# Expert layer: two tiles routed before the first one-hots, dots of gathered rows spread over two tiles, four row buffers

## The chip, the cores and the metric

The kernel runs on 1 core of one Trainium2 chip. The metric is the device time in microseconds (us) of one launch. Engines are named as in the profile: PE is TensorE (PEld its weight loads), DVE is VectorE, ACT is ScalarE, POOL is GpSimd, SP issues transfers. All arithmetic is in float32; large products are split into a high and a low part (three matmuls in place of one).

## The reference, cut to what matters

The program runs two blocks of layers on 512 tokens of width 1024. The change lies in the last layer, a product-key expert layer (PEER) with 16,384 experts; each token takes 128 of them.

```python
def peer_ffn(h, wq, subkeys, u, v):
    q = (xt @ wq).reshape(T, PEER_HEADS, 2, PEER_HALF)
    s = jnp.einsum('thpc,hpnc->thpn', q, subkeys)
    s_top, i_top = lax.top_k(s, PEER_TOPK)
    cand = s_top[:, :, 0, :, None] + s_top[:, :, 1, None, :]
    cand_idx = i_top[:, :, 0, :, None] * PEER_N_KEYS + i_top[:, :, 1, None, :]
    best, pos = lax.top_k(cand.reshape(T, PEER_HEADS, -1), PEER_TOPK)
    experts = jnp.take_along_axis(cand_idx.reshape(T, PEER_HEADS, -1), pos, axis=-1)
    gates = jax.nn.softmax(best, axis=-1)
    ...
        ub = u[eb]
        vb = v[eb]
        act = jax.nn.gelu(jnp.einsum('cd,ced->ce', xb, ub)) * gb
        return jnp.einsum('ce,ced->cd', act, vb)
```

## The kernel before

The 512 tokens are four tiles of 128. Tile 0 and half of tile 1 (`HT = 64` tokens) are computed sparsely, from gathered rows of `u`; the other 320 tokens (`TU`) densely: products with all 16,384 rows of `u`, in 128 blocks of 128 experts, times a matrix G that holds the gates of the chosen experts and zeros elsewhere. Nothing of the dense products depends on the routing, so the first 66 blocks (`NA`) are computed during the routing and stored to memory (`up_store`, here "a fill": 24 matmuls at line 192, one GELU at line 1247, one store at line 1248; its weights come from SP, are split by ACT at line 115 and by POOL at line 118).

The part that the change touches is the last third of `peer`:

- `route(t, out)` (line 1257) finds for tile t the best 16 of each head's candidates and their expert numbers as two digits, nearly all of it on DVE; six operations of it (lines 1299, 1303, 1307, twice) are large, 128x2048 elements. Its PE part is none; one exponential runs on ACT.
- `transposed(res)` (line 1326) turns the two digits and the gates of a tile round: three PE transposes (line 1329) and a copy on ACT (line 1331) into `rt`.
- `onehots(t, rt, steps, pace, fills)` (line 1390) builds G for one tile in 32 groups of four tokens. A group needs two one-hot tiles, `oh1` (line 1405 on DVE, in one group of four line 1403 on POOL) and `oh2` (lines 1408 on DVE and 1410 on ACT, or 1413 and 1414 on DVE), four PE matmuls (line 1417) and a copy into `stage` on ACT (line 1419). After a group the function takes steps from the generator `steps` until they have used `pace` units per group, and it issues its share of `fills` fills. Tiles 2 and 3 are then written to memory (line 1433).
- `udots_begin`, `udots`, `udots_end` (lines 1350 to 1388) compute the sparse half of tile 1. `udots_begin` makes the row numbers `idx1` (line 1356, behind two small PE matmuls of line 1344) and the normalised tokens `xn1` (line 1367, behind the PE matmuls of line 1362 and a load of a gain row, line 1364). Then 64 gathers of 128 rows each (512 KB, `ugather`, line 1347, an indirect transfer issued by POOL) fetch rows of `u` into the row buffers `ub`, and 64 dots on DVE (line 1374) multiply them with `xn1` and sum. `xn1` and the three buffers lie in the dead activations `xT`, 4 KB per partition each.

The order of the work is the program's order: a Tile scheduler fills each engine's queue from it, each queue runs in order, and an operation waits for what it reads and for whoever still uses what it writes. The calls at the end of the section, in the order in which they stand (lines 1452 to 1460):

```python
        fill(FIRST)
        ...
        for _ in route(2, res):
            pass
        onehots(2, transposed(res), between2(), 3.1, 20)
        onehots(3, rts[0], between3(), 2.9, 20)
        onehots(1, rts[1], route(0, r0), 1.45, 12)
        fill(NA)
```

`between2` (line 1440) routes tile 1, starts the dots and routes tile 3 beside the one-hots of tile 2; `between3` (line 1448) computes the 64 dots beside those of tile 3; tile 0 is routed beside those of tile 1. After this the dense products run to the end of the launch.

Of the kernel before, what the change touches and what calls it, by code (L numbers as in the profile page):

```python
# [14 lines left out]
ALU = mybir.AluOpType  # L15
# [4 lines left out]
D = 1024  # L20
P = 128
# [6 lines left out]
FIRST = 14  # L28
# [15 lines left out]
def body(tc, A, out, upto=None, dbg=None):  # L44
    nc = tc.nc
# [1108 lines left out]
    def peer(norm):  # L1154
        H, L = norm.h, norm.l
        TD, TU, HT = 384, 320, 64
# [75 lines left out]
        def b_(name, shape, bufs=1, dt=F32):  # L1232
            return pgb.tile(list(shape), dt, name=name, tag=name, bufs=bufs)
# [18 lines left out]
        def fill(n):  # L1252
            for _ in range(n):
                if ahead:
                    up_store(ahead.popleft())
# [80 lines left out]
        xn1, ub = flat[:, 0:D], [flat[:, (n + 1) * D:(n + 2) * D] for n in range(3)]  # L1336
# [9 lines left out]
        def ugather(k):  # L1346
            G.indirect_dma_start(out=ub[k % 3], out_offset=None, in_=urows,  # L1347
                                 in_offset=bass.IndirectOffsetOnAxis(ap=idx1[:, k:k + 1], axis=0))

        def udots_begin(res):  # L1350
# [13 lines left out]
            nc.scalar.dma_start(ub[2], A["ffn_norm_row"].to_broadcast([P, D]))  # L1364
            for hf in range(2):
                o = slice(hf * 512, (hf + 1) * 512)
                V.tensor_tensor(xn1[:, o], pxs[hf], ub[2][:, o], ALU.mult)
            ugather(0)
            ugather(1)

        def udots():
            for k in range(HT):
                u = ub[k % 3]
                V.scalar_tensor_tensor(u, u, 1.0, xn1, op0=ALU.mult, op1=ALU.mult, accum_out=dval[:, k:k + 1])  # L1374
                if k + 2 < HT:
                    ugather(k + 2)
                yield 1.4
# [12 lines left out]
        def onehots(t, rt, steps, pace, fills):  # L1390
# [3 lines left out]
            for q4 in range(32):  # L1394
# [5 lines left out]
                oh1 = b_("oh1", (P, 4, P), bufs=3)  # L1400
# [5 lines left out]
                oh2 = b_("oh2", (P, 4, P), bufs=3)  # L1406
# [32 lines left out]

        def between2():  # L1440
            yield from route(1, r1)
            udots_begin(r1)
            yield 3.0
            res = []
            yield from route(3, res)
            rts.append(transposed(res))

        def between3():
            yield from udots()
            rts.append(udots_end(r1))  # L1450

        lsplit[:] = [G]
        fill(FIRST)
        res = []
        for _ in route(2, res):
            pass
        onehots(2, transposed(res), between2(), 3.1, 20)
        onehots(3, rts[0], between3(), 2.9, 20)
        onehots(1, rts[1], route(0, r0), 1.45, 12)
# [336 lines left out]
```

## Time and profile before

| | |
|---|---|
| median of 3 runs | 2993.33 us (2985.81 to 2994.05) |
| the profiled execution | 2987.53 us, its span 2985.8 us |
| PE busy | 2857.4 us, 96% of the span |
| DVE, ACT, POOL busy | 2006.1, 1430.8, 1244.9 us |
| granted clock of PE, mean | 0.984 |
| transfers | 516.84 MB, 173 GB/s |

The rows used below come from the page of the profiled execution and from queries of its trace. A row of a stretch (a window of the span) gives each engine's busy time (PE, PEld, DVE, ACT, POOL) and, in brackets, its instructions, then the granted clock as a share of the full 2.4 GHz, the busy share of the DMA engines and GB/s. A row of waits gives who waited, for whom, the total, how often and the longest. A row of a timeline gives start, duration, engine, line and operation, and in square brackets the idle time of the engine ahead of it with its releaser. Matmuls are pipelined, so the duration of one is longer than the distance to the next.

### The profile page before, as it was taken

To read this page: it belongs to the slowest core of one execution; us is meant where nothing else is said; L and a number is where in the kernel's file an instruction comes from. 1 tells how busy PE (TensorE), PEld (TensorE's weight loads), DVE (VectorE), ACT (ScalarE), POOL (GpSimd) and SP (SyncE) were. 2 spreads that over 40 slices of the span, in tenths; PEclk is the share of its full clock that TensorE was granted. 3 is DMA by queue.
4 is the path that set the end of the run, shared out by engine and by line. 5 is a ranking of instruction groups with operands and counts; after the bars stand their busy time and mean duration, and the time that the engine had idled before them with its cause. 6 is when DMAs were issued, how large, how long until landed. Compare 5 with 4: busy or idle time off the path is not lost.

```text
span 2985.8 us, 47379 instructions
## 1 busy us (share of the span) xinstructions
PE 2857.4 (96%) x18255; PEld 2561.3 (86%) x18255; DVE 2006.1 (67%) x3484; ACT 1430.8 (48%) x2464; POOL 1244.9 (42%) x800
## 2 busy tenths in 40 slices
PE   8999999999999999999999998866799999999998
PEld 8999999988899998875788898866788888888887
DVE  4656645567664647447655778677867888887887
ACT  4454433366542435425444346634575545555555
POOL 4124323342232324105312355577655555555553
PEclk9999999999999999999999999987999999999999
DMA  4213322331132233221242344789758999999996
GB/s 134 66 51 100 100 97 95 100 99 43 64 100 93 99 100 108 85 71 41 71 130 88 107 137 142 201 277 290 214 223 328 353 364 348 356 358 351 349 352 238
DMA packets 216002, 516.84 MB, mean 173 GB/s; under 512 B 83032, under 2 KB 120280, under 8 KB 198880
## 3 DMA queue, kind: packets, MB, share of 16 engines
q1 hardware_dynamic: 172320, 325.29, 33.1%
q0 software_dynamic: 27648, 167.78, 14.9%
q10 hardware_dynamic: 15808, 20.74, 2.0%
q8 instruction: 143, 2.34, 0.3%
q14 instruction: 83, 0.68, 0.1%
HBM read 481.96 MB, written 31.78 MB: 172 GB/s over the span
## 4 chain that ended last, share of the span: by engine, by line
PE 77%; DVE 6%; issue 5%; POOL 5%; ACT 3%; DMA 3%; SPq 0%; ACTq 0%; DVEq 0%; POOLq 0%
PE mm L192 60%; PE ax L192 11%; POOL wl L118 2%; POOL xT L1347 2%; PE ax L1417 1%; DMA xT<-in_uv_dram,idx 1%; DVE scr L1530 1%; ACT wh L115 1%; POOL oh L1403 1%; DVE xt L1539 1%; PE mm L1027 1%; PE ax L1211 1%; DMA w<-in_pv_dram 1%; DVE xT L1374 0%; PE ax L997 0%
## 5 line engine op out<-in xcount | busy, mean ns | idle before, releaser
L118 POOL TENSOR_TENSOR wl<-w,wh 128x1024 fp32r<-128x1024 f32 x265 | 665.0, 2511 | 956.3 <-ACT wh L115 769.7
L115 ACT ACTIVATE wh<-w 128x1024 fp32r<-128x1024 f32 (+1 forms) x530 | 559.1, 1057 | 717.6 <-PE mm L192 443.2
L192 PE MATMUL mm<-sh,wh 128*128 128x256 f32 (+2 forms) x3144 | 746.9, 303 | 7.1 <-ACT sh L225 6.4
L192 PE MATMUL mm<-sl,wh 128*128 128x256 f32 (+2 forms) x3144 | 743.5, 302 | 1.9 <-POOL sl L205 1.7
L192 PE MATMUL mm<-sh,wl 128*128 128x256 f32 (+2 forms) x3144 | 742.1, 301 | 1.1 <-DVE wl L118 1.1
L192 PEld LDWEIGHTS mm<-sh,wh 128*128 128x128 f32 (+1 forms) x3144 | 498.1, 188 | 40.4 <-ACT sh L225 6.4
L192 PEld LDWEIGHTS mm<-sl,wh 128*128 128x128 f32 (+1 forms) x3144 | 497.0, 188 | 32.3 <-POOL sl L205 2.0
L192 PEld LDWEIGHTS mm<-sh,wl 128*128 128x128 f32 (+1 forms) x3144 | 497.5, 188 | 30.4 <-DVE wl L118 1.4
L118 DVE TENSOR_TENSOR wl<-w,wh 128x1024 fp32r<-128x1024 f32 (+1 forms) x265 | 339.4, 1281 | 234.0 <-ACT wh L115 228.5
L192 PE MATMUL mm<-xnh,wh 128*128 128x320 f32 x784 | 256.3, 327 | 2.0 <-ACT wh L115 2.0
L192 PE MATMUL mm<-xnh,wl 128*128 128x320 f32 x784 | 252.0, 321 | 3.0 <-POOL wl L118 3.0
L192 PE MATMUL mm<-xnl,wh 128*128 128x320 f32 x784 | 252.9, 323 | 0.0
L1417 PE MATMUL ax<-oh,oh 128*128 128x128 f32 x768 | 130.9, 308 | 80.9 <-ACT oh L1410 42.8
L1417 PEld LDWEIGHTS ax<-oh,oh 128*128 128x128 f32 x768 | 112.3, 208 | 98.0 <-ACT oh L1410 52.0
L285 DVE TENSOR_TENSOR xT<-xT,mm 128x512 f32<-128x512 f32 x80 | 54.7, 686 | 163.3 <-PE mm L192 163.3
L192 PE MATMUL mm<-wh,ah 128*128 128x512 f32 x384 | 152.4, 397 | 9.5 <-ACT ah L1572 9.4
L192 PEld LDWEIGHTS mm<-xnh,wh 128*128 128x128 f32 x784 | 155.7, 199 | 3.7 <-ACT wh L115 2.2
L192 PEld LDWEIGHTS mm<-xnh,wl 128*128 128x128 f32 x784 | 155.1, 198 | 3.6 <-POOL wl L118 3.5
L192 PEld LDWEIGHTS mm<-xnl,wh 128*128 128x128 f32 x784 | 155.4, 198 | 1.3
L1419 ACT ACTIVATE stage<-ax 128x512 f32<-128x512 f32 x96 | 103.5, 1094 | 108.8 <-PE ax L1417 108.3
L192 PE MATMUL mm<-wh,al 128*128 128x512 f32 x384 | 151.9, 396 | 0.0
L192 PE MATMUL ax<-wh,ah 128*128 128x512 f32 x384 | 150.1, 391 | 0.0
(501 smaller groups left out, 5516.4 us busy)
## 6 DMA issues: line engine op xcount, KB each, us to landing
w<-in_pu_dram SPq DMA_DIRECT2D x128, 512.0 KB, 4.3
w<-in_pv_dram SPq DMA_DIRECT2D x128, 512.0 KB, 7.1
w<-in_up_dram SPq DMA_DIRECT2D x88, 512.0 KB, 3.5
w<-in_down_dram SPq DMA_DIRECT2D x48, 512.0 KB, 3.5
Gd<-stage SPq DMA_DIRECT2D x32, 512.0 KB, 8.1
gm<-Gd SPq DMA_DIRECT2D x128, 128.0 KB, 7.3
Hd<-gel ACTq DMA_DIRECT2D x66, 160.0 KB, 3.5
gst<-Hd SPq DMA_DIRECT2D x66, 160.0 KB, 7.2
```

The costliest lines, as they stand in the source:

```text
L115: SC.activation(h[:, :n], w[:, :n], AF.Copy)
L118: ins = eng.tensor_tensor(l[:, :n], w[:, :n], h[:, :n].bitcast(F32), ALU.subtract)
L192: PE.matmul(ps[:, c:c + w], lhsT=a, rhs=b[:, c:c + w], start=start and c == 0 and a is lh and b is rh, stop=stop and c + w == n and a is ll)
L285: V.tensor_tensor(xT[:, c], xT[:, c], ps, ALU.add)
L1027: PE.matmul(po[e * 64:e * 64 + 64, c * P:], lhsT=vs[:, c, hd * 64:hd * 64 + 64], rhs=at[:, c * P:], start=c == 0, stop=c == 3)
L1211: PE.matmul(pss[:, t * P:(t + 1) * P], lhsT=q[:, t * P:(t + 1) * P], rhs=sk, start=True, stop=True)
L1347: G.indirect_dma_start(out=ub[k % 3], out_offset=None, in_=urows, in_offset=bass.IndirectOffsetOnAxis(ap=idx1[:, k:k + 1], axis=0))
L1403: G.tensor_scalar(oh1[:, k], iot, rt[:, 0, 4 * q4 + k:4 * q4 + k + 1], None, op0=ALU.is_equal)
L1417: PE.matmul(pg[:, k * P:(k + 1) * P], lhsT=oh1[:, k], rhs=oh2[:, k], start=True, stop=True)
L1419: SC.activation(st[:, :, o:o + 4].rearrange("p j t -> p t j"), pg.rearrange("p (t j) -> p t j", t=4), AF.Copy)
L1530: V.scalar_tensor_tensor(scr, uv[:, :D], 1.0, xn, op0=ALU.mult, op1=ALU.mult, accum_out=d)
L1539: V.scalar_tensor_tensor(xt0, uv[:, D:], d, xt0, op0=ALU.mult, op1=ALU.add)
```

## The change

Tile 1 is routed first, then `udots_begin` is called and tile 2 is routed, all before the first one-hots; 21 fills (`FIRST`) stand ahead of this in place of 14, and 16 and 17 fills beside tiles 2 and 3 in place of 20 and 20. The dots are one generator that is drawn on beside tile 2's one-hots (with the routing of tile 3, 1.3 units of dots for one of routing) and beside tile 3's (with the routing of tile 0, 1.6 to one, and then the rest). Nothing is left to do beside tile 1's. `xn1` gets a tile of its own, so that `xT` holds four row buffers, and a gather is issued three dots ahead of its use in place of two. `oh1` and `oh2` have four buffers each in place of three.

```diff
-FIRST = 14
+FIRST = 21
...
-        xn1, ub = flat[:, 0:D], [flat[:, (n + 1) * D:(n + 2) * D] for n in range(3)]
+        xn1, ub = b_("xn1", (P, D)), [flat[:, n * D:(n + 1) * D] for n in range(4)]
...
         def ugather(k):
-            G.indirect_dma_start(out=ub[k % 3], out_offset=None, in_=urows,
+            G.indirect_dma_start(out=ub[k % 4], out_offset=None, in_=urows,
...
-            nc.scalar.dma_start(ub[2], A["ffn_norm_row"].to_broadcast([P, D]))
+            nc.scalar.dma_start(ub[3], A["ffn_norm_row"].to_broadcast([P, D]))
             for hf in range(2):
                 o = slice(hf * 512, (hf + 1) * 512)
-                V.tensor_tensor(xn1[:, o], pxs[hf], ub[2][:, o], ALU.mult)
-            ugather(0)
-            ugather(1)
+                V.tensor_tensor(xn1[:, o], pxs[hf], ub[3][:, o], ALU.mult)
+            for k in range(3):
+                ugather(k)
 
         def udots():
             for k in range(HT):
-                u = ub[k % 3]
+                u = ub[k % 4]
                 V.scalar_tensor_tensor(u, u, 1.0, xn1, op0=ALU.mult, op1=ALU.mult, accum_out=dval[:, k:k + 1])
-                if k + 2 < HT:
-                    ugather(k + 2)
+                if k + 3 < HT:
+                    ugather(k + 3)
                 yield 1.4
...
-                oh1 = b_("oh1", (P, 4, P), bufs=3)
+                oh1 = b_("oh1", (P, 4, P), bufs=4)
...
-                oh2 = b_("oh2", (P, 4, P), bufs=3)
+                oh2 = b_("oh2", (P, 4, P), bufs=4)
...
+        dots = udots()
+
+        def with_dots(steps, share):
+
+            owed = 0.0
+            for c in steps:
+                yield c
+                owed += share * c
+                while owed >= 1.4:
+                    owed -= 1.4
+                    d = next(dots, None)
+                    if d is not None:
+                        yield d
+
         def between2():
-            yield from route(1, r1)
-            udots_begin(r1)
-            yield 3.0
             res = []
-            yield from route(3, res)
+            yield from with_dots(route(3, res), 1.3)
             rts.append(transposed(res))
 
         def between3():
-            yield from udots()
+            yield from with_dots(route(0, r0), 1.6)
+            yield from dots
             rts.append(udots_end(r1))
 
         lsplit[:] = [G]
         fill(FIRST)
+        for _ in route(1, r1):
+            pass
+        udots_begin(r1)
         res = []
         for _ in route(2, res):
             pass
-        onehots(2, transposed(res), between2(), 3.1, 20)
-        onehots(3, rts[0], between3(), 2.9, 20)
-        onehots(1, rts[1], route(0, r0), 1.45, 12)
+        onehots(2, transposed(res), between2(), 2.35, 16)
+        onehots(3, rts[0], between3(), 2.6, 17)
+        onehots(1, rts[1], iter(()), 0.0, 12)
```

How the instructions now stand, at three places. A row gives the line of the kernel, the operation, what it writes from what it reads, and its size; x3 at a row's end is three in a row; a number behind a name tells tiles of one name apart.

On PE, at the end of the fills that stand ahead of the first one-hots; before, only the transposes of tile 2 (line 1329) stood between the last fill's matmul and the first one-hot product:

```order
L192 MATMUL mm<-xnh,wl 128x320
L1329 MATMUL ax<-ident,e_18383 128x128
L1329 MATMUL ax<-ident,e_18388 128x128
L1329 MATMUL ax<-ident,gt 128x128
L1417 MATMUL ax<-oh_18405,oh_18403 128x128 x2
```

and now the matmuls of `udots_begin` stand there too, behind 21 fills; the first of them (line 1344) makes the row numbers from the digits of tile 1, the last of them (line 1329) need the routing of tile 2:

```order
L192 MATMUL mm<-xnh,wl 128x320
L1344 MATMUL ax<-pf,ident 64x64 x2
L1344 MATMUL ax<-prcol,ident 64x2 x2
L1362 MATMUL ax<-ident,xT 64x128 x8
L1362 MATMUL mm<-ident,xT 64x128 x8
L1329 MATMUL ax<-ident,e_18741 128x128
L1329 MATMUL ax<-ident,e_18746 128x128
L1329 MATMUL ax<-ident,gt 128x128
L1417 MATMUL ax<-oh_18763,oh_18761 128x128 x4
```

The matmuls of lines 1344 and 1362 have moved from the middle of tile 2's one-hots to a place ahead of them.

On DVE, in the routing of tile 2, now: the row numbers (line 1356, `idx`, which reads what PE's line 1344 wrote) stand behind the small operations of this routing and ahead of its six large ones:

```order
L1317 TENSOR_TENSOR gt<-gt,sm 128x128
L1278 CAST pf<-bi 128x128
L1356 TENSOR_SCALAR idx_17833<-ax 128x64
L1357 COPY rdup<-ax 128x2
L1289 SCALAR_TENSOR_TENSOR fi<-pf,fi 128x128
L1290 SCALAR_TENSOR_TENSOR fj<-fi,pf 128x128
L1292 SCALAR_TENSOR_TENSOR fw<-fi,pf 128x128
L1299 TENSOR_TENSOR oh<-fi,ax 128x2048
L1293 SCALAR_TENSOR_TENSOR fj<-fw,fj 128x128
L1303 TENSOR_TENSOR oh<-oh,ax 128x2048
L1367 TENSOR_TENSOR xn_17832<-ax,xT 128x512
L1367 TENSOR_TENSOR xn_17832<-mm,xT 128x512
```

Behind these rows come four more large operations, four small ones and then the first one-hot. Before, nothing in the routing of tile 2 read anything of PE.

On DVE, in the middle of the dots, before (line 1374 is a dot; the one-hots are tile 3's):

```order
L1374 SCALAR_TENSOR_TENSOR xT,dval<-xT 128x1024 x2
L1414 TENSOR_TENSOR oh_20259<-mm,rt 128x512
L1374 SCALAR_TENSOR_TENSOR xT,dval<-xT 128x1024 x2
L1405 TENSOR_TENSOR oh_20275<-rt,ax 128x512
L1374 SCALAR_TENSOR_TENSOR xT,dval<-xT 128x1024
L1408 TENSOR_TENSOR oh_20277<-rt,ax 128x512
```

and now, where the one-hots are tile 2's and the other rows belong to the routing of tile 3:

```order
L1374 SCALAR_TENSOR_TENSOR xT,dval<-xT,xn_17832 128x1024 x2
L1408 TENSOR_TENSOR oh_19431<-rt,ax 128x512
L1303 TENSOR_TENSOR oh<-oh,ax 128x2048
L1405 TENSOR_TENSOR oh_19444<-rt,ax 128x512
L1413 TENSOR_TENSOR mm<-rt,ax 128x512
L1405 TENSOR_TENSOR oh_19494<-rt,ax 128x512
L1414 TENSOR_TENSOR oh_19446<-mm,rt 128x512
L1374 SCALAR_TENSOR_TENSOR xT,dval<-xT,xn_17832 128x1024 x2
L1408 TENSOR_TENSOR oh_19496<-rt,ax 128x512
L1307 TENSOR_REDUCE e_19508<-oh 128x128
```

The dots stand further apart: 29 of the 64 now lie ahead of the last one-hots of tile 2, the other 35 ahead of the last of tile 3.

## Rows read from the trace of the kernel before

**Rows 1.** The page: busy time of PE over the span.
```profile
PE 2857.4 (96%) x18255; PEld 2561.3 (86%) x18255; DVE 2006.1 (67%) x3484; ACT 1430.8 (48%) x2464; POOL 1244.9 (42%) x800
```

**Rows 2.** Stretches: first fills, then the one-hots of tiles 2, 3 and 1.
```profile
1757.00:1802.00 45.00, 43.87 (x300) 43.62 (x299) 29.35 (x101) 21.50 (x32) 30.56 (x14) 1.00 0.64 198
1802.00:1925.00 123.00, 108.58 (x752) 104.63 (x753) 106.64 (x272) 83.09 (x143) 68.27 (x57) 0.94 0.54 158
1925.00:2130.00 205.00, 140.76 (x766) 129.46 (x765) 146.87 (x198) 80.90 (x137) 152.13 (x116) 0.83 0.85 271
2130.00:2214.00 84.00, 76.51 (x556) 73.19 (x555) 68.01 (x166) 69.17 (x125) 44.88 (x40) 1.00 0.56 157
```

**Rows 3.** Waits of DVE in tile 3's stretch, 1925 to 2130.
```profile
DVE xT L1374 <- DMA xT<-in_uv_dram,idx: 57.6, 33, 7.9
```

**Rows 4.** Waits of DVE in tile 2's stretch, 1802 to 1925.
```profile
DVE oh L1405 <- ACT rt L1331: 15.6, 1, 15.6
DVE oh L1405 <- PE ax L1417: 13.5, 5, 5.8
```

**Rows 5.** The chain that ended last, from the first fills (start us, us, what).
```profile
1752.73 47.77 PE mm L192 x326
...
1801.86 0.39 ACT rt L1331
```

**Rows 6.** DVE's timeline: first and last operation of tile 2's routing, first one-hot.
```profile
1758.09 0.41 DVE L1259 CAST ax<-ti 128x256 f32<-128x256 uint32 x1
...
1782.05 2.29 DVE L1303 TENSOR_TENSOR oh<-oh,ax 128x2048 f32<-128x2048 f32 x1
1784.37 2.29 DVE L1307 TENSOR_REDUCE e<-oh 128x128 f32<-128x2048 f32 x1
1802.27 0.69 DVE L1405 TENSOR_TENSOR oh<-rt,ax 128x512 f32<-128x512 f32 x1 [15.61 <-ACT rt L1331]
```

**Rows 7.** Row buffers (tile xT), 1925 to 2130: waits (us, times); gathers' landing.
```profile
  issue: 6.7, 27
...
  POOL xT L1347: 41.8, 30
...
DMA to landing us min/median/max: 4.2/6.0/8.4
```

**Rows 8.** DVE's groups in tile 3's stretch: the dots (busy us, mean ns).
```profile
L1374 DVE SCALAR_TENSOR_TENSOR xT<-xT 128x1024 f32<-128x1024 f32 x62 | 104.7, 1695 | 57.8 <-DMA xT<-in_uv_dram,idx 57.6
```

**Rows 9.** Timeline about 1956: a dot beside a POOL split, undisturbed ones, one-hots.
```profile
1955.35 2.36 POOL L118 TENSOR_TENSOR wl<-w,wh 128x1024 fp32r<-128x1024 f32 x1
...
1956.42 2.38 DVE L1374 SCALAR_TENSOR_TENSOR xT<-xT 128x1024 f32<-128x1024 f32 x1 [0.90 <-DMA xT<-in_uv_dram,idx]
...
1962.57 0.68 DVE L1405 TENSOR_TENSOR oh<-rt,ax 128x512 f32<-128x512 f32 x1
1963.17 0.69 DVE L1413 TENSOR_TENSOR mm<-rt,ax 128x512 f32<-128x512 f32 x1
...
1970.81 1.22 DVE L1374 SCALAR_TENSOR_TENSOR xT<-xT 128x1024 f32<-128x1024 f32 x1
...
1971.95 1.22 DVE L1374 SCALAR_TENSOR_TENSOR xT<-xT 128x1024 f32<-128x1024 f32 x1
```

**Rows 10.** POOL's groups in tile 3's stretch, 1925 to 2130.
```profile
L1347 POOL DMA_INDIRECT xT<-in_uv_dram,idx x61 | 68.8, 1127 | 50.3 <-DVE xT L1374 41.8 <-issue 6.7 <-PE mm L192 0.8
L118 POOL TENSOR_TENSOR wl<-w,wh 128x1024 fp32r<-128x1024 f32 x22 | 53.0, 2410 | 0.5
L1403 POOL TENSOR_SCALAR oh<-iot,rt 128x128 f32<-128x128 f32 x33 | 30.8, 943 | 0.5 <-ACT rt L1331 0.3
```

**Rows 11.** POOL's groups in tile 2's stretch, 1802 to 1925.
```profile
L118 POOL TENSOR_TENSOR wl<-w,wh 128x1024 fp32r<-128x1024 f32 x19 | 45.8, 2420 | 36.0 <-ACT wh L115 35.9
```

**Rows 12.** The chain: one group's PE products at full clock.
```profile
2146.90 0.89 PE ax L1417 x8
```

**Rows 13.** Timeline: the end of the last fill's matmuls.
```profile
2213.50 0.31 PE L192 MATMUL mm<-xnh,wl 128*128 128x320 f32 x1
```

## The prediction

> **What bounds the kernel now.** I read the page first. PE is busy 96% of the span [rows 1], so the kernel can only gain where PE waits or runs at a lower clock. Of the page's slices it is those of the expert layer's one-hots that drop. I cut that stage into stretches [rows 2]: in the first fills PE is busy 43.87 of 45 us at full clock; beside tile 2's one-hots 108.58 of 123; beside tile 3's only 140.76 of 205, at a granted clock of 0.83; beside tile 1's 76.51 of 84. The reader should see that 205 us of tile 3 hold as many one-hots as the 123 us of tile 2, and much the same number of fills.
>
> The waits tell why. In tile 3's stretch DVE stands 57.6 us for gathered rows [rows 3], and POOL in turn stands 41.8 us for dots that have not yet given a row buffer back [rows 7]. It is one ring: a gather takes 6.0 us to land (median, 4.2 to 8.4 [rows 7]), its dot about 1.2 [rows 9], and with three buffers a gather may start only when the dot three places earlier is done. Since all one-hots stand in DVE's queue among the dots, they wait too, and PE behind them. In tile 2's stretch DVE loses 15.6 us at the start, because the transposes of tile 2 stand on PE behind the fills, and 13.5 us for one-hot buffers that PE has not yet read [rows 4].
>
> Everything after the stage is the same in both kernels; I take it to move as a block. So the sum is: when does the first one-hot of tile 2 start (before: 1802.3 [rows 6]), how long do tiles 2 and 3 take (before: to 2130, 327.7 us), how long does tile 1 take (before: 2130 to the last fill's end at 2213.8 [rows 13], 83.8 us).
>
> **The start.** 326 matmuls of the first fills take 47.77 us [rows 5], 0.1465 us each, 3.52 us for a fill of 24. By the order, 20.58 fills now stand in that place: 72.4 us from 1752.7, to 1825.1. DVE needs 28.6 us for one routing (1758.1 to the end of the last large operation, 1786.7 [rows 6]). Two would be done at 1815 and be hidden. But in DVE's queue the row numbers stand in the middle of tile 2's routing, and they read PE's line 1344, which stands behind all 21 fills. So DVE arrives there at about 1797 and stands until 1825.7. Behind it are six large operations at 2.3 us start to start [rows 6], 13.5 us, two `xn1` halves at 0.6 and eight small operations at some 0.25: 17 us, to about 1843. PE has nothing to do from 1826.5 on but the transposes that wait for this. Transposes and copy cost 1.8 us (before: 1800.5 to 1802.3 [rows 5, 6]), and I allow 1 us for small operations that POOL holds up: first one-hot at **1846**, 43.7 us later than before. The gain row lands well before `xn1` needs it; if it did not, 2 to 4 us more. Bounds: 1844 to 1850. Of this, 24.6 us are fills that only moved; the other 19 are PE standing still, and they have to be earned back.
>
> **Tiles 2 and 3.** The same work as before lies in this stretch: 64 groups of one-hots, 64 dots, two routings (3 and 0 in place of 1 and 3). From 327.7 us go:
> - 2 us for `idx1` and `xn1`, now ahead of it.
> - The wait for gathers, 57.6 us [rows 3]. With four buffers a gather waits for the dot four places earlier, and the dots are thinned out. Adding DVE's own starts along the new order (a dot 1.15, a one-hot operation 0.60 [rows 9], a large one 2.3 [rows 6]), four dots in a row span 9.8 us at the least and 12.8 in the median. A gather needs 1.2 for that dot and 6.0 to land, 7.2 us. That leaves 2.6 to 5.6 us for POOL to come round to it; a split of weights on POOL holds it for 2.41 [rows 10]. Most gathers land in time; I leave 5 us, bounds 0 and 25.
> - The wait for one-hot buffers, 13.5 us [rows 4]. Four buffers and a slower pace of one-hots: 5 left, bounds 0 and 13.5.
> - The stretching of dots. 62 dots took 104.7 us [rows 8]; at 1.22 undisturbed they would take 75.6, so 29 us are lost. The timeline shows to what: the dot at 1956.42 takes 2.38 us beside a POOL split that ends at 1957.71, while undisturbed ones start 1.14 apart [rows 9]. In tile 3's stretch POOL's tensor work was 53.0 + 30.8 us of 205 [rows 10], about 73 without its own stretching (33 one-hots at 0.6), 36%. Now the dots meet 33 splits and 64 POOL one-hots, 79 + 38 = 117 us of about 270, 43%: 29 becomes 36, **7 us more**. Bounds: 14 less (dots that no longer start on a buffer's return meet POOL at other moments) to 14 more.
>
> The Trainium skill says that a VectorE instruction with two SBUF inputs and a GpSimd instruction that reads SBUF exclude each other for a whole instruction, the first one wins (SBUF — State Buffer, Who interferes with whom). By that rule the dots, which read two such tiles, are the wrong work to lay beside more POOL work: it speaks against this change, and the 7 us stand. Without it the 29 us would stay and the gain be 7 larger. The 2.38 us row agrees with the rule.
>
> A second rule bears on the gathers: the Trainium skill has a POOL transfer cost about 2.0 us plus its bytes at 436 GB/s (DMA: Bandwidth & Descriptors, Anatomy of one DMA). By that estimate 512 KB land in 3.2 us; then no gather would be late in the new order and the 5 us left above be 0. The trace has 6.0 us, and I stay with it.
>
> Together: 327.7 − 2 − 57.6 + 5 − 13.5 + 5 + 7 = **271.6 us**, to 2117.6. A check from below: 64 groups of 2.25 DVE operations at 0.60 are 86 us, 64 dots at 1.15 are 74, two routings 57: 217 us with nothing in the way, plus 36 of stretching and some 16 of waits. PE's own work there, 33 fills at 3.52 and 64 groups at 0.89 [rows 12], is 173 us at full clock, 208 at tile 3's 0.83 [rows 2]: it stays covered by DVE, and so costs nothing as long as DVE takes longer.
>
> **Tile 1.** By the order 12.4 fills and 32 groups remain on PE: 43.6 + 28.5 = 72 us. DVE no longer has a routing there (28.6 of its 68.01 us [rows 2]), so PE sets the pace; ACT, busy 69.17 us before with the exponential of a routing, is just below it. I take **76 us**, bounds 72 and 84, to 2193.6.
>
> **Sum.** The stage ends at 2193.6 in place of 2213.8: 20.2 us earlier. The profiled execution took 2987.53 us for a span of 2985.8, so it would give 2967.3; the median of the runs is 5.8 us above that execution, and 2993.3 − 20.2 = **2973 us** is what I predict for the median.
>
> **The rivals.**
> - *POOL becomes the bound (slower).* In the new stretch POOL has 64 gathers at 1.13, 33 splits at 2.41 and 64 one-hots at up to 0.94 [rows 10], 72 + 80 + 60, and about 0.25 us of issue per gather (6.7 over 27 [rows 7]), 16: 228 us. If its splits also wait for ACT as they did in tile 2's stretch, 35.9 us in 123 [rows 11], that is 79 us in 271, and gathers queue behind those waits: 307 us. The stage would end at 1846 + 307 + 76 = 2229, 15 us later than before, **3008 us**. It decides from 292 us on (2213.8 − 76 − 1846). Against it: such a wait is mostly POOL being ahead with its splits, and a gather that stands behind one has 2.6 to 5.6 us to spare. For it: POOL's queue is in order, and 33 splits now lie among 64 gathers. Chance 0.12.
> - *The waits shrink but stay (no change).* Gathers are late by 15 to 25 us and the one-hot wait stays at 10 to 13.5: in place of 5 and 5 that is 15 to 28.5 us more in the stretch, so 5 us faster to 8 us slower, **2988 to 3002 us**. This is where the late start is just earned back. For it: the landing time reaches 8.4 us [rows 7], and the shortest four dots leave no room for that and a split. Chance 0.13.
> - *The new order does better (larger gain).* No late gathers, no one-hot waits, the stretching 15 us less than now, tile 1 at 72: 20 + 5 + 5 + 14 + 4 = 48 us, **2945 us**. For it: the dots come no longer right behind a gather's landing. Against it: all of this at once was seen nowhere in the trace. Chance 0.17 for over 33 us.
> - *The change does not do what it says.* Half of this is in the forecast: two tiles are routed ahead of the one-hots, but the second half of the second stands behind the fills.
>
> **How the numbers follow.** The forecast, a gain of 9 to 33 us, has 0.58. About 0.3%, 9 us, is what a measurement of this kernel can tell from no change. Faster by more than that: 0.58 + 0.17 = 0.75. Within it: 0.13. Slower: 0.12, the POOL case. The range goes from the larger gain's end, 2945, to 3000, near the upper end of no change; the slower case lies outside it.
>
> **What would show it.** In the new profile the first one-hot of tile 2 should start near 1846, with DVE standing some 28 us before `idx1` (waiting for line 1344) and PE some 18 us before line 1329. DVE's wait for gathers should fall below 10 us; the mean of a dot should stay at 1.7 to 1.8 us; tiles 2 and 3 should take 262 to 282 us and tile 1 72 to 80. I am wrong if the wait for gathers stays above 25 us, if POOL is full through the stretch, or if PE's clock falls so far there (below 173 / 292 = 0.59) that PE sets the pace.

## The result and the profile after

The changed kernel takes 2964.89 us (median of 5 runs, 2963.02 to 2987.88); on the same chip the kernel before takes 2994.05 us (median of 5, 2985.81 to 3005.99). The ratio is 0.992, with a 95% interval of 0.9895 to 0.9945: faster by about 24 us by the ratio and 29.2 us by the medians, where 20.2 us and a median of 2973 us were forecast.

The profiled execution of the changed kernel took 2987.88 us, 23 us above its median, with a span of 2986.1 us: it came to the first fills 12.4 us later than that of before, in code that both kernels share. So I compare stages here, cut at the same four points in every trace:

- the start: from the start of the last matmul of line 1211 (the product that the routing reads) to the start of the first one-hot of tile 2;
- tiles 2 and 3: from there to the multiplication on DVE that ends `udots_end`;
- tile 1: from there to the first transpose of the next stage on PE (line 1507 of the kernel before, 1522 of the changed one), which is 7 to 10 us beyond the end of the last fill, where the prediction ended it.

| kernel | start | tiles 2 and 3 | tile 1 | sum | median us | ratio, 95% interval |
|---|---|---|---|---|---|---|
| before | 49.8 | 326.8 | 94.8 | 471.4 | 2994.05 | |
| changed | 96.3 | 276.0 | 85.0 | 457.3 | 2964.89 | 0.992 [0.9895, 0.9945] |
| e1 the same, other chip | 96.0 | 266.9 | 84.9 | 447.8 | 2973.77 | 0.9924 [0.99, 0.9948] |
| e2 eight fills later | 78.1 | 267.4 | 84.9 | 430.4 | 2952.55 | 0.9874 [0.9851, 0.9897] |
| e3 three row buffers | 95.4 | 268.6 | 87.6 | 451.6 | 2970.08 | 0.9916 [0.99, 0.9933] |
| e4 dots from PSUM | 95.5 | 266.1 | 86.2 | 447.8 | 2962.26 | 0.9904 [0.9878, 0.9929] |
| e5 dots not spread | 95.8 | 288.1 | 83.4 | 467.3 | 2988.3 | 0.9985 [0.9976, 0.9994] |
| e6 before, four row buffers | 49.8 | 328.0 | 97.3 | 475.1 | 2984.66 | 0.9976 [0.9967, 0.9985] |
| e7 stores spread | 96.1 | 260.7 | 84.9 | 441.7 | 2958.25 | 0.9887 [0.9872, 0.9902] |
| e8 = e4 + e7 | 95.1 | 237.8 | 83.6 | 416.5 | 2936.89 | 0.9824 [0.981, 0.9837] |
| e9 = e8 + e2 | 78.2 | 242.9 | 83.6 | 404.7 | 2919.05 | 0.9759 [0.9746, 0.9773] |
| e10 three one-hot buffers | 95.6 | 267.7 | 85.0 | 448.3 | 2964.2 | 0.9906 [0.9892, 0.9921] |
| e11 = e9, dots not spread | 78.1 | 259.4 | 84.2 | 421.7 | 2943.92 | 0.9834 [0.9807, 0.9861] |

Stages come from the profiled execution of each kernel, medians from all its runs. The ratio is against the kernel before on the same chip.

The stretches of the changed kernel, with the columns of [rows 2]: up to the first one-hot of tile 2, tiles 2 and 3, tile 1 to the end of the last fill.

```profile
1750.00:1861.00 111.00, 91.04 (x616) 86.88 (x614) 71.60 (x294) 42.77 (x61) 61.29 (x28) 0.93 0.53 173
1861.00:2137.00 276.00, 210.57 (x1298) 197.09 (x1299) 251.17 (x462) 154.47 (x264) 203.45 (x156) 0.89 0.78 239
2137.00:2216.00 79.00, 78.03 (x585) 76.67 (x585) 45.05 (x74) 68.95 (x128) 47.34 (x44) 1.00 0.68 190
```

In tiles 2 and 3 DVE is now busy 251.17 of 276 us (91%); before it was 253.5 of 328 (106.64 + 146.87, 77% [rows 2]): the same work with fewer holes. In the last row PE is full, 78.03 of 79 us, where it had 76.51 of 84.

The start, by the waits of DVE from 1757 to 1861, and of PE in the same window:

```profile
DVE pf L1278 <- PE ax L1344: 28.4, 1, 28.4
...
DVE xn L1367 <- DMA xT<-in_ffn_norm_row_dram: 3.6, 1, 3.6
```

```profile
PE ax L1329 <- DVE e L1307: 18.7, 2, 11.4
```

DVE's timeline shows the end of this chain, from the release by line 1344 to the first one-hot:

```profile
1839.01 0.23 DVE L1278 CAST pf<-bi 128x128 f32<-128x128 uint32 x1 [28.35 <-PE ax L1344]
1839.15 0.21 DVE L1356 TENSOR_SCALAR idx<-ax 128x64 int32<-128x64 f32 x1
...
1848.39 0.69 DVE L1367 TENSOR_TENSOR xn<-ax,xT 128x512 f32<-128x512 f32 x1 [3.64 <-DMA xT<-in_ffn_norm_row_dram]
...
1861.19 0.69 DVE L1405 TENSOR_TENSOR oh<-rt,ax 128x512 f32<-128x512 f32 x1 [1.31 <-ACT rt L1331]
```

DVE stands one operation ahead of the row numbers: line 1278 writes `pf`, a tile with one buffer into which line 1353 has put tile 1's expert numbers, and line 1344 has yet to read them. The row numbers (line 1356) then follow without a wait, so moving them alone to a later place would not have shortened this. The second wait, 3.64 us, is for the gain row. Its load writes into a row buffer in `xT`, which the matmuls of line 1362 read until 1840.82, and it is issued right after them, as ACT's timeline shows:

```profile
1840.87 0.34 ACTq L1364 DMA_DIRECT2D xT<-in_ffn_norm_row_dram  x1
```

It landed 7.4 us later.

Tiles 2 and 3, by the waits of DVE from 1861 to 2137; they answer to [rows 3, 4]:

```profile
DVE xT L1374 <- DMA xT<-in_uv_dram,idx: 14.2, 8, 7.8
DVE oh L1405 <- ACT rt L1331: 4.7, 2, 3.4
...
DVE oh L1405 <- PE ax L1417: 1.0, 1, 1.0
```

And POOL's waits there, to be held against [rows 7, 11]:

```profile
POOL wl L118 <- ACT wh L115: 29.3, 9, 7.7
POOL xT L1347 <- DVE xT L1374: 14.6, 9, 3.9
```

The groups of DVE and of POOL in this stretch, which answer to [rows 8, 10]:

```profile
L1374 DVE SCALAR_TENSOR_TENSOR xT<-xT,xn 128x1024 f32<-128x1024 f32 x64 | 109.4, 1716 | 14.2 <-DMA xT<-in_uv_dram,idx 14.2
```

```profile
L118 POOL TENSOR_TENSOR wl<-w,wh 128x1024 fp32r<-128x1024 f32 x32 | 81.3, 2543 | 29.7 <-ACT wh L115 29.3
L1347 POOL DMA_INDIRECT xT<-in_uv_dram,idx x60 | 68.8, 1146 | 40.7 <-DVE xT L1374 14.6 <-issue 5.6 <-DVE bv L1189 5.4
L1403 POOL TENSOR_SCALAR oh<-iot,rt 128x128 f32<-128x128 f32 x64 | 53.7, 851 | 10.6 <-ACT rt L1331 10.4
```

The wait for gathered rows fell from 57.6 us in 33 pieces to 14.2 in 8, and POOL's wait for row buffers from 41.8 to 14.6 us. The dots themselves cost what they did, 1716 ns in the mean against 1695.

### The profile page after: what moved, and what is told of

The parts are those of the page before. It is cut to its first block, busy times and chain, and to the rows that moved or that the text cites. A ratio compares the mean times of both kernels' runs of the same rounds, so it can differ in the third digit from the quotient of the medians.

```text
span 2986.1 us, 47341 instructions
## 1 busy us (share of the span) xinstructions
PE 2862.3 (96%) x18255; PEld 2568.0 (86%) x18255; DVE 2007.0 (67%) x3484; ACT 1431.1 (48%) x2464; POOL 1253.8 (42%) x800
## 5 line engine op out<-in xcount | busy, mean ns | idle before, releaser
L192 PE MATMUL mm<-xnh,wh 128*128 128x320 f32 x784 | 253.5, 323 | 0.0
L192 PE MATMUL mm<-xnl,wh 128*128 128x320 f32 x784 | 249.2, 318 | 0.0
L1417 PE MATMUL ax<-oh,oh 128*128 128x128 f32 x768 | 121.6, 300 | 66.3 <-ACT oh L1410 40.9
L561 POOL TENSOR_TENSOR y<-y 128x512 f32<-128x512 f32 x44 | 56.8, 1291 | 225.7 <-ACT y L560 225.7
```

Source lines behind the costliest of these rows:

```text
L192: PE.matmul(ps[:, c:c + w], lhsT=a, rhs=b[:, c:c + w], start=start and c == 0 and a is lh and b is rh, stop=stop and c + w == n and a is ll)
L561: G.tensor_tensor(val, val, gate, ALU.mult)
L1417: PE.matmul(pg[:, k * P:(k + 1) * P], lhsT=oh1[:, k], rhs=oh2[:, k], start=True, stop=True)
```

## The experiments

My theory at this point: the stretch of tiles 2 and 3 became shorter because the dots lie further apart, so that a gather has landed when its dot comes. Rivals: the fourth row buffer alone does it, or the fourth one-hot buffers. Two costs looked open to recovery: the late start, and the stretched dots.

**e1: the same kernel on another chip.**

> The changed kernel once more, for a second profile. Its first profiled execution was 23 us longer than the median of its own runs, so it is the less typical one. My steps expect: 2960 to 2970 us; in the trace the first one-hot of tile 2 at 1846 to 1850, DVE standing about 28 us for the row numbers, PE about 19 us for the routing of tile 2, DVE's wait for gathers 5 to 15 us, tiles 2 and 3 in 268 to 278 us, tile 1 in 76 to 80. The rival (the gain comes from something else than the stage) expects the stage to end where it ended before, about 2214, in an execution of 2965.

Measured: 2973.77 us (2961.5 to 2983.4, 6 runs), ratio 0.9924; the median lies above the 2960 to 2970 us that I expected. Tiles 2 and 3 take 266.9 us, 9 less than in the first trace and a little below my 268. DVE's wait for gathers, from 1862 to 2129:

```profile
DVE xT L1374 <- DMA xT<-in_uv_dram,idx: 6.5, 7, 1.7
```

The gain repeats. Two traces of one kernel differ by 9 us in this stretch, so a smaller difference between two stretches below is not, by itself, read as an effect.

**e2: 13 fills ahead of the routing and 8 behind the row numbers.**

```diff
-        fill(FIRST)
+        fill(13)
         for _ in route(1, r1):
             pass
         udots_begin(r1)
+        fill(FIRST - 13)
```

> The change, with the eight last of the 21 fills moved behind the start of the dots, so that PE reaches the row numbers after 13 fills. DVE's order stays the same, and so does PE's behind the transposes. My reading (the late start is lost time, 17 to 19 us of PE standing): first one-hot at about 1829 instead of 1846, and all of it reaches the end: 2944 to 2952 us, 0.5 to 0.7% below the change. Rival (the stage is paced by gathers or by POOL from there on, and an early start is eaten by later waits): 2958 to 2968 us, with DVE's wait for gathers up by 10 us or more.

Measured: the start falls from 96.0 to 78.1 us and the two tiles keep their length (267.4). In the stretches of this kernel PE is full from the start on, 75.60 of 78 us:

```profile
1751.00:1829.00 78.00, 75.60 (x540) 74.73 (x538) 63.41 (x225) 37.28 (x51) 53.53 (x26) 1.00 0.66 216
1829.00:2096.00 267.00, 205.21 (x1297) 192.79 (x1297) 249.02 (x462) 154.91 (x264) 205.69 (x157) 0.92 0.81 251
```

The 19 us that PE stood still in the changed kernel's start were a matter of order alone. DVE still stands ahead of the first one-hot, 9.24 us in place of 1.31, since the transposes of tile 2 now stand behind the eight fills on PE. The median, 2952.55 us, is 21.2 below e1's on the same chip, just above the 2944 to 2952 that I expected; the stage is 17.4 us shorter.

**e3: three row buffers, gathers two ahead.**

```diff
-            G.indirect_dma_start(out=ub[k % 4], out_offset=None, in_=urows,
+            G.indirect_dma_start(out=ub[k % 3], out_offset=None, in_=urows,
...
-                if k + 3 < HT:
-                    ugather(k + 3)
+                if k + 2 < HT:
+                    ugather(k + 2)
```

> The change with three row buffers and gathers issued two dots ahead, as before; everything else as changed. Theory 1 (thinning the dots out is what removed the wait): three dots in a row span 7.4 us at the least and 9.2 or more in most places, against 7.2 that a gather and a dot need, so DVE's wait for gathers rises from about 14 to 20 to 35 us and the time to 2972 to 2985. Theory 2 (the fourth buffer is what removed it): the wait comes back to 45 us or more, 2990 to 3005 us. If neither matters, the time stays at 2965.

Measured: 2970.08 us, nothing lost that can be told from e1, and two tiles of 268.6 us; I had expected a loss. DVE's waits from 1852 to 2120:

```profile
DVE xT L1374 <- DMA xT<-in_uv_dram,idx: 18.3, 16, 4.9
DVE oh L1405 <- ACT rt L1331: 3.8, 2, 2.5
```

The gathers are late by 18.3 us in place of 6.5, yet the stretch ends 1.7 us later. The dots cost 13.0 us less (95.8 against 108.8) and all of DVE's work 6.6 us less (246.0 against 252.6); that a dot which starts later met POOL less often is my reading and not shown. The rival that the fourth row buffer alone brings the gain is out.

**e4: one operand of the dots in PSUM.** `xn1` stays in the two PSUM tiles in which its product is made, so each dot becomes two halves of 512.

```diff
-                V.tensor_tensor(xn1[:, o], pxs[hf], ub[3][:, o], ALU.mult)
+                V.tensor_tensor(pxs[hf], pxs[hf], ub[3][:, o], ALU.mult)
+            xn1.extend(pxs)
...
-                V.scalar_tensor_tensor(u, u, 1.0, xn1, op0=ALU.mult, op1=ALU.mult, accum_out=dval[:, k:k + 1])
+                for hf, acc in enumerate((dval, dvh)):
+                    o = slice(hf * 512, (hf + 1) * 512)
+                    V.scalar_tensor_tensor(u[:, o], u[:, o], 1.0, xn1[hf], op0=ALU.mult, op1=ALU.mult, accum_out=acc[:, k:k + 1])
...
+            V.tensor_tensor(dval, dval, dvh, ALU.add)
```

> The change with the normalised tokens left in PSUM, so that a dot reads one SBUF tile and one PSUM tile; each dot becomes two of 512 elements with an addition of the two sums at the end. If what stretches the dots is POOL's tensor work beside instructions with two SBUF inputs: dots take 2 x 0.6 us everywhere, POOL's one-hots fall from 0.85 to 0.6 us, some 30 us of DVE and POOL time come back in tiles 2 and 3 and the time falls to 2935 to 2955 us. If the stretching comes from something else (the transfers writing the row buffers, say), the halves stay stretched and the time is 2962 to 2975.

Measured: the stretching is gone, the time isn't. Two groups of DVE, and one of POOL, from 1844 to 2110:

```profile
L1377 DVE SCALAR_TENSOR_TENSOR xT<-xT,mm 128x512 f32<-128x512 f32 x64 | 43.3, 677 | 0.0
L1377 DVE SCALAR_TENSOR_TENSOR xT<-xT,ax 128x512 f32<-128x512 f32 x64 | 43.2, 676 | 14.6 <-DMA xT<-in_uv_dram,idx 14.6
```

```profile
L1407 POOL TENSOR_SCALAR oh<-iot,rt 128x128 f32<-128x128 f32 x64 | 38.5, 616 | 10.8 <-ACT rt L1331 10.3
```

A dot now costs 1.35 us every time (no half took more than 0.689 us), 86.5 us in all against 108.8 in e1, and POOL's one-hots take 616 ns in place of 851. Yet the two tiles take 266.1 us, against 266.9. Something else ends them. What it is stands in the waits of ACT and of PE in the same window:

```profile
ACT wh L115 <- DMA w<-in_pu_dram: 27.3, 5, 11.5
```

```profile
PE ax L1421 <- ACT oh L1414: 58.3, 21, 13.2
```

ACT stands 27.3 us for weights that have not landed, its one-hots (line 1414) stand behind that in its queue, and PE waits for them, 13.2 us at the longest. Why weights are late is seen on SP, which issues them; its timeline in this kernel:

```profile
1900.01 28.45 SPq L1437 DMA_DIRECT2D Gd<-stage  x7
1928.56 29.63 SPq L110 DMA_DIRECT2D w<-in_pu_dram  x7
```

The last seven of the eight stores of half a tile's G (line 1433 of the changed kernel, 1437 here) follow each other for 28.45 us, and in that time no weights are asked for. The chain that ended last, by line within the stretch, for e1 and for this kernel:

```profile
by line: DVE xT L1374 20.2%; SPq L1433 17.2%; DMA w<-in_pu_dram 7.4%; PE ax L1417 7.2%; PE mm L192 7.0%; DVE oh L1405 5.6%; DVE oh L1414 4.0%; DVE mm L1413 3.6%; DVE oh L1408 3.5%; DMA xT<-in_uv_dram,idx 3.4%; issue 2.7%; DVE fw L1292 2.3%;
```

```profile
by line: PE mm L192 25.6%; SPq L1437 22.5%; PE ax L1421 16.8%; DMA w<-in_pu_dram 8.2%; issue 5.3%; DVE xT L1377 3.6%; ACT oh L1414 2.5%; ACT gel L1247 2.0%; SPq L110 1.7%; DVE oh L1409 1.6%; ACT wh L115 1.4%; DVE oh L1412 1.1%; ACT L1313 1.
```

The dots fell from 20.2% of the chain to 3.6%, and SP's stores rose from 17.2% to 22.5%. That points to two limits of much the same height, and e7 and e8 are made to test it. A rival is that the two PSUM tiles which `xn1` now keeps are missed elsewhere; e8 keeps them too.

**e5: the spreading undone.** All 64 dots beside tile 3 again; the routing ahead, the buffers and the fills stay as changed.

```diff
-            yield from with_dots(route(3, res), 1.3)
+            yield from route(3, res)
...
-        onehots(2, transposed(res), between2(), 2.35, 16)
-        onehots(3, rts[0], between3(), 2.6, 17)
+        onehots(2, transposed(res), between2(), 1.05, 16)
+        onehots(3, rts[0], between3(), 3.9, 17)
```

> The change with all 64 dots beside the one-hots of tile 3 (and beside the routing of tile 0), none beside tile 2's; four row buffers and the two tiles routed ahead stay. If thinning the dots out removed the wait for gathers: 64 dots in one tile leave three in a row about 5 to 7 us apart, below the 7.2 a gather and a dot need, so DVE waits 30 us or more for gathers again, tiles 2 and 3 take 285 to 305 us, and the time is 2980 to 3000. If routing ahead and the buffers carry the gain: the wait stays under 20 us, tiles 2 and 3 under 275, the time at 2962 to 2972.

Measured: 2988.3 us, ratio 0.9985: nearly all of the gain is given back. The two tiles take 288.1 us. DVE's waits from 1848 to 2136:

```profile
DVE xT L1374 <- DMA xT<-in_uv_dram,idx: 23.9, 12, 4.4
DVE oh L1405 <- ACT rt L1331: 9.6, 2, 8.2
DVE oh L1405 <- PE ax L1417: 3.5, 4, 1.4
```

The wait for gathers is below the 30 us that I gave as the least, since part of the dots is still mixed with tile 0's routing. All of DVE's waits together are 39.7 us against e1's 14.6, 25 us more, and its busy time is 6 us less; that accounts for 19 of the 21 us by which the stretch is longer than e1's.

The stretch is still 38.7 us shorter than in the kernel before. That part came with what e5 keeps: seven of 40 fills moved out of the stretch (24.6 us of PE's work), tile 0's routing laid among the dots, and the buffers; no run separates these. With tile 1, 11.4 us shorter, it makes 50.1 us, against a start that is 46.0 us longer. So routing ahead about pays for itself, and the gain that is left is about what the spreading brings.

**e6: the kernel before with the fourth row buffer alone** (the lines of the change on `ub`, `xn1` and `ugather`).

```diff
-        xn1, ub = flat[:, 0:D], [flat[:, (n + 1) * D:(n + 2) * D] for n in range(3)]
+        xn1, ub = b_("xn1", (P, D)), [flat[:, n * D:(n + 1) * D] for n in range(4)]
...
-                if k + 2 < HT:
-                    ugather(k + 2)
+                if k + 3 < HT:
+                    ugather(k + 3)
```

> The kernel before with only the fourth row buffer (and gathers three dots ahead). After the run with three buffers, in which the fourth was worth 2 us in the changed order, I expect it to matter here, where dots stand 1.2 to 2.9 us apart: three gathers in flight in place of two let a dot come every 2.4 us at best instead of 3.2, so DVE's wait falls from 57.6 to 25 to 40 us, POOL's wait for dots from 41.8 to below 20, and the time to 2965 to 2980. Rival (the gathers are limited by what the DMA engines move, 0.85 busy in that stretch): the wait stays above 50 us and the time at 2988 to 2998.

Measured: 2984.66 us, ratio 0.9976, some 7 us faster than the kernel before and between the two theories. DVE's wait for gathers, from 1805 to 2133:

```profile
DVE xT L1374 <- DMA xT<-in_uv_dram,idx: 44.8, 21, 6.9
```

It falls by 12.8 us from [rows 3], but in the profiled execution, which took 8.5 us more than the median, the two tiles take 328.0 us as before (326.8). DVE's busy time rose by 9 us (261.4 against 252.5), 4 of them in the dots, whose mean went from 1680 to 1752 ns. A fourth buffer at the same density of dots is worth some 7 us by the ratio and nothing that this trace's stretch shows.

**e7: one store per group in place of eight in a row.**

```diff
+                if stores:
+                    j0, c0, half = stores.popleft()
+                    nc.sync.dma_start(Gd[j0:j0 + 16, :, c0:c0 + HT].rearrange("j i t -> i j t"),
+                                      stage[:, half, j0:j0 + 16])
                 if q4 % 16 == 15 and t > 1:
                     c0 = (t - 2) * P + (q4 // 16) * HT
-                    for j0 in range(0, P, 16):
-                        nc.sync.dma_start(Gd[j0:j0 + 16, :, c0:c0 + HT].rearrange("j i t -> i j t"),
-                                          st[:, j0:j0 + 16])
+                    stores.extend((j0, c0, q4 // 16) for j0 in range(0, P, 16))
```

> The change with the stores of a half tile (eight of 512 KB, issued in a row by SP, 23 to 32 us in which no weights are loaded) issued one per group of one-hots instead. In the run with the dots in PSUM, 28 us of DVE work went away and tiles 2 and 3 took the same 266 us, while ACT stood 27 us for weights behind these stores. If DVE (with its stretched dots) and SP's stores are two limits of equal height, this alone gives little: tiles 2 and 3 in 262 to 268 us, time 2958 to 2972. If the stores alone set the pace: 245 to 255 us and 2945 to 2955.

**e8: e4 and e7 together.**

> Both: dots that read the tokens from PSUM, and stores one per group. If the two are limits of equal height, the 28 us of DVE time now come through: tiles 2 and 3 in 236 to 250 us, time 2935 to 2950 from the same late start. If something else holds the stretch at 266 us (gathers, PE, or the pace of the steps), nothing moves: 2958 to 2968.

Measured, on one chip: e7 2958.25 us with two tiles of 260.7 us (262 to 268 expected), e8 2936.89 us with 237.8. The four stretches, with neither remedy, PSUM alone, stores alone and both, are 266.9, 266.1, 260.7 and 237.8 us: the remedies save 0.8 and 6.2 us alone, neither more than two traces of one kernel differ by, and 29.1 together. The chain within the stretch, for e7 and for e8:

```profile
by line: DVE xT L1374 23.1%; PE mm L192 13.4%; PE ax L1419 9.3%; DVE oh L1407 6.7%; DMA xT<-in_uv_dram,idx 6.3%; DVE mm L1415 4.9%; DVE oh L1416 4.6%; DVE oh L1410 4.6%; issue 3.4%; DVE fw L1292 2.3%; DVE oh L1303 1.7%; DVE oh L1299 1.7%; D
```

```profile
by line: DVE xT L1377 18.2%; PE mm L192 15.9%; PE ax L1423 11.0%; issue 7.3%; DVE oh L1411 7.0%; DVE oh L1420 4.7%; DVE oh L1414 4.7%; DVE mm L1419 4.5%; DMA xT<-in_uv_dram,idx 3.1%; ACT oh L1416 2.6%; ACT gel L1247 1.6%; ACT stage L1425 1.
```

With the stores spread, SP has left the chain and DVE's dots lead it; DVE is then busy 249.2 of 260 us. With both, neither SP's stores nor late weights appear in what is shown of the chain, no wait of ACT for weights is left (27.3 us in e4), and DVE is busy 225 of 238 us:

```profile
1849.00:2087.00 238.00, 199.44 (x1310) 187.33 (x1311) 225.21 (x593) 156.05 (x267) 172.65 (x157) 0.95 0.88 279
```

**e9: e8 with the fills split as in e2.**

> The change with both remedies of the last run (dots with one operand in PSUM, stores of the stage one per group) and with 13 of the 21 fills ahead of the routing and 8 behind the row numbers of tile 2. If the late start, the stretching and the run of stores are three separate costs, the gains add up: from the last fill's rows to the first one-hot about 78 us in place of 95, the two tiles 236 to 242 us as in the run with both remedies, the stage 396 to 402 us and the median 2916 to 2925 us. If the 8 fills behind the row numbers only pay back work that PE would have done beside the two tiles, their start is earlier and their stretch longer by as much: 250 to 257 us and a median of 2932 to 2940 us.

Measured: 2919.05 us (2916.31 to 2921.82), ratio 0.9759. The start falls by 16.9 us, of which the two tiles take back 5.1 (242.9 against 237.8, a little past the 242 that I gave as the most). Of these, 3.9 us are a longer wait of DVE for the exponential of a routing (line 1313, 6.6 us against 2.7). The three costs are separate, and their gains add up to within those 5 us. This is the fastest kernel here, 71 us below the kernel before on its chip (2990.54).

**e10: three one-hot buffers of each kind in place of four** (`bufs=3` for `oh1` and `oh2`).

> The change with three one-hot buffers of each kind in place of four. If DVE's one-hots, now 8 of every 16 groups' work apart from the dots, run far enough ahead of PE and POOL for the fourth buffer to matter, DVE waits longer for their release: two tiles 270 to 276 us against 267, and the median 2968 to 2980 us. If three are enough, as they were for the row buffers within some 2 us, two tiles 265 to 269 us and the median within 5 us of the change's own, 2962 to 2974 us.

Measured: 2964.2 us and two tiles of 267.7, as with four. DVE's wait for one-hot buffers, from 1863 to 2131:

```profile
DVE oh L1405 <- PE ax L1417: 2.0, 1, 2.0
```

The rival of the one-hot buffers is out.

**e11: e9 with the dots not spread** (the edit of e5).

> The last kernel but one (dots with one operand in PSUM, stores one per group, 13 fills ahead and 8 behind) with all 64 dots laid beside tile 3 again. If the spreading is still what carries the two tiles when the two other limits are gone, DVE waits for gathered rows again for 15 us or more and the two tiles take 258 to 268 us in place of 243: a median of 2934 to 2944 us. If the spreading was worth its 20 us only because stretched dots and late gathers fell on the same tile, the undisturbed dots and four row buffers do without it: two tiles of 240 to 250 us and a median of 2917 to 2927 us.

Measured: 2943.92 us, two tiles of 259.4 us. DVE's waits from 1836 to 2096:

```profile
DVE oh L1411 <- ACT rt L1331: 16.8, 2, 9.2
DVE xT L1377 <- DMA xT<-in_uv_dram,idx: 16.3, 12, 3.1
```

In e9 the wait for gathers is 0.5 us. The spreading is worth 16.5 us of the stretch here and 21 in the changed kernel: it isn't a remedy for stretched dots or late weights, but for gathers that stand too close.

## Why the prediction was right

The forecast was a gain of 20.2 us; the two measurements of the same kernel gave 0.8% each, about 23 us. It was right for the reasons it gave, with three terms off in size and one limit unseen; that this limit lay close to the forecast length of tiles 2 and 3 was luck.

- **The start.** DVE stood 28.4 us for line 1344 (forecast some 28) and PE 18.7 us ahead of line 1329 (18). The first one-hot is 46.5 us later in its stage, not 43.7. The step that failed is "the gain row lands well before `xn1` needs it": DVE stood 3.6 us for it, within the 2 to 4 that the prediction gave for that case, because its load was issued only after line 1362. The prediction also put the wait at the row numbers themselves; it stood at line 1278, one operation ahead, for the tile `pf`. Both wait for line 1344, so the time came out. e2 confirms the reading that these 19 us were not needed: it takes 17.9 of the start away.
- **The wait for gathers.** Forecast 57.6 to 5; measured 14.2 in one trace and 6.5 in the other, inside the bounds, near or a little above the value. e5, e6 and e3 together show that the distance between dots does most of it and the buffer less: with the old density a fourth buffer left 44.8 us of 57.6, with the new density three buffers left 18.3 and cost 1.7 us of the stretch, and with the dots partly drawn together again (e5) 23.9 came back. A gather landed in 6.1 us in the median, as before [rows 7], and in 12.0 at the latest. From the transfers into the row buffers, 1861 to 2137:

```profile
DMA to landing us min/median/max: 4.2/6.1/12.0
```

  The Trainium skill's price for a POOL transfer (DMA: Bandwidth & Descriptors, Anatomy of one DMA), 3.2 us by the estimate in the prediction, is not borne out: no gather landed in less than 4.2 us, and some waits stayed.
- **The wait for one-hot buffers.** Forecast 13.5 to 5, measured 1.0. Of the two reasons given, "four buffers and a slower pace", only the pace holds: with three buffers (e10) it is 2.0.
- **The stretching of dots.** Forecast a mean of 1.7 to 1.8 us, measured 1.716. At 1.22 each the 64 dots lose 31.7 us, against 36 forecast (29 scaled from 36% to 43%, which is nearer to 35). The longest is this one, from DVE's and POOL's timelines of the changed kernel:

```profile
1963.31 5.77 DVE L1374 SCALAR_TENSOR_TENSOR xT<-xT,xn 128x1024 f32<-128x1024 f32 x1
```

```profile
1963.30 4.69 POOL L118 TENSOR_TENSOR wl<-w,wh 128x1024 fp32r<-128x1024 f32 x2
```

  POOL's two splits begin 0.01 us ahead of the dot and end at 1967.99; the dot ends 1.09 us later, about the time of an undisturbed one. The Trainium skill's rule that such instructions exclude each other as a whole and the first one wins (SBUF — State Buffer, Who interferes with whom) agrees, and e4 agrees from the other side: with one input in PSUM the halves take 677 ns in the mean.
- **Tiles 2 and 3.** Forecast 271.6 us, measured 276.0 and 266.9. The step that doesn't hold is the check from below: it added the stretching and the waits to DVE's work as if DVE alone set the pace. By that, e4 would have saved its 22 us; it saved 0.8. SP's runs of eight stores, which no term of the sum had, held the stretch at nearly the same length, and DVE's waits hid behind them. The sum came out because the two limits were about equal, and nothing in the prediction said that they would be.
- **Tile 1.** Forecast 76 us to the end of the last fill; in the new trace that is 2137.2 to 2215.5, 78.3 us, with PE full as forecast. From there to the next stage's transposes it is 6.7 us in place of 10.1: 3.4 us that the prediction had not foreseen. What follows moved as a block (763.9 us to the end of the span against 761.9).
- **The sum.** The stage is 14.1 us shorter in the first pair of traces and 23.6 with e1's, around the 20.2 forecast.
- **The rivals.** POOL did not become the bound: it was busy 203.45 of 276 us and its splits waited 29.3 us for ACT, not the 79 that I had scaled up from [rows 11]. That fits the argument against that rival, that such a wait is POOL being ahead with its splits: DVE's wait for gathers fell all the same. "The waits shrink but stay" asked for 15 to 25 us of late gathers and 10 to 13.5 for one-hot buffers: 14.2 and 1.0. The larger gain exists, but not in the change as it stands: it asked for less stretching and fewer waits, of which the prediction said that "all of this at once was seen nowhere in the trace", and it took e8's two remedies together to reach it.

What stays open: whether three buffers of both kinds at once would still be enough, which of the things that e5 keeps made its two tiles 38.7 us shorter than before, and why PE took longer for the same matmuls ahead of the stage in three of the traces (last section).

## What to carry to other kernels

Where an in-order queue consumes transfers out of a small ring of buffers, first spread the consumers among other work of that queue, and only then add buffers: here the spreading carried 16 to 21 us, and a fourth buffer at the old density brought some 7. When a remedy visibly works (the dots were no longer stretched) and the time stays, follow the chain to the limit of the same height and remove both; alone they brought 0.8 and 6.2 us, together 29.1. Look at each engine's queue for work that waits in front of work that others need: eight fills moved behind a small matmul brought 17.9 us of the start, and eight stores in a row held weights back for more than 20 us.

## What the runs showed of the hardware

PE did not get through identical code ahead of the stage at one rate: the start of the stage lies between 1748.6 and 1767.3 us in the traces. Between 300 and 600 us, the stretch of the kernel before, of the changed one, of e5:

```profile
300.00:600.00 300.00, 298.46 (x2631) 298.06 (x2630) 164.58 (x172) 111.05 (x136) 93.50 (x57) 1.00 0.30 99
```

```profile
300.00:600.00 300.00, 300.00 (x2550) 300.00 (x2549) 159.22 (x164) 104.11 (x128) 89.78 (x55) 1.00 0.30 94
```

```profile
300.00:600.00 300.00, 298.46 (x2631) 298.06 (x2630) 164.72 (x171) 111.17 (x137) 96.99 (x59) 1.00 0.32 100
```

In the second PE is full and gets through 2550 matmuls in place of 2631, with fewer operations on every other engine too, at a granted clock of 1.00 in all three; the traces of e1 and e10 are like the second (2549 and 2550). These matmuls, of 256 columns, start 0.118 us apart there and 0.113 in the first, while those of 320 columns in the first fills (about 1770 us) start 0.147 apart in both. So it isn't the whole of PE's work that takes longer. By an estimate, 81 matmuls at 0.118 us, this is 9.5 of the 12.4 us by which this trace comes later to the first fills. No run here tells why.

A run of eight stores took SP 22.75 us (changed kernel) and weights came only behind it:

```profile
1925.19 22.75 SPq L1433 DMA_DIRECT2D Gd<-stage  x8
1948.03 32.87 SPq L110 DMA_DIRECT2D w<-in_pu_dram  x7
```

The 32 stores of this kernel took SP 2.73 us each in the median, 0.38 at the least and 5.65 at the most, where issuing a load of weights (line 110) took 0.33 in the median. With one store per group (e8) the median was 0.95 us. So a loop of eight that looks free in the program is a long wall in SP's queue.
